# AdaLN products moved to the boundaries between sublayers, and the last AdaLN chunk computed in two halves

## The chip, the cores and the metric

The kernel runs on one core of a Trainium2 chip. The core has five engines that work side by side, each through its own instruction queue: TensorE (PE in the profile; its weight loads are shown as PEld), VectorE (DVE), ScalarE (ACT), GpSimd (POOL) and SyncE (SP, which here only issues DMAs). PE writes its results to PSUM; everything else lives in SBUF. The metric is the device time of one execution in microseconds (us); lower is better.

## What is computed

The reference is a trunk of two layers over 256 latent and 256 context tokens of width 1024. Each layer has a mixer (mLSTM, differential attention and a Fourier branch, merged by gates) and an FFN, and before each of these the stream is normed and modulated. The part that matters here is where the modulation comes from (AdaLN): a vector per stream (latent, context) times a 1024 x 6144 matrix per layer, cut in six.

```python
for l in range(DEPTH):
    ml = jnp.split((s_lat @ w_ada[l] + b_ada[l])[:, None, :], 6, axis=-1)
    mc = jnp.split((s_ctx @ w_ada[l] + b_ada[l])[None, None, :], 6, axis=-1)
    hl = _modulate(_rmsnorm(xl, norm_g[l, 0]), ml[0], ml[1])
    hc = _modulate(_rmsnorm(xc, norm_g[l, 0]), mc[0], mc[1])
    yl, yc = _mixer(hl, hc, ...)
    xl = xl + ml[2] * yl
    xl = xl + ml[5] * _swiglu(_modulate(_rmsnorm(xl, norm_g[l, 1]), ml[3], ml[4]), w_ffn_in[l], w_ffn_out[l])
    if need_ctx:
        xc = xc + mc[2] * yc
        xc = xc + mc[5] * _swiglu(_modulate(_rmsnorm(xc, norm_g[l, 1]), mc[3], mc[4]), w_ffn_in[l], w_ffn_out[l])
```

The second layer (l = 1) needs its mixer output and FFN for the 256 latent tokens alone.

## The kernel before

**Jobs.** The work is a list, `prog`, of jobs. A job is one weight tile of 512 KB: its DMA (`load`, L204), its split into a high part on ACT (`split_hi`, L214) and a low part on DVE (`split`, L224), and its matmuls, three for each f32 product (high by high, high by low, low by high). `run_all` goes through the list: before job i runs, the loads of all jobs up to i + 7 are written out (`AHEAD_LOAD`, L288), and the splits of up to three jobs ahead. Raw weight tiles have four buffers, so the load of job n + 4 waits until job n is split. Within a job, `yield` marks places where the side work of the moment (`side`, `tick`) may write out one of its steps, at a rate given by a number of steps over a number of jobs.

**What sets the order.** SP issues its DMAs in the order in which the program writes them. The other engines' instructions are ordered by a list scheduler, which takes whatever it holds to be ready, in the written order where several are; inside `chain` (L594 to L658) DVE and ACT too keep the written order, but not PE.

**Buffers.** A unit (`unit()`) is 4 KB a partition, and there are 32 of them, for the stream, the normed tokens, the activations and the AdaLN weights. The small PSUM tiles (`side_ps()`) have four buffers.

**AdaLN.** Layer 0's first chunk is made in the opening. The other five chunks of 2048 columns (layer 0: s = 1, 2; layer 1: s = 0, 1, 2) are objects of the class `Ada`. A chunk has eight products, one for each 128 rows k of the matrix; a product is four matmuls (j = 0 to 3) of the 128x32 vector columns by 128x512 of weights, each into its own 32 rows of one PSUM tile, at L363. Its weights are two units of 512 KB, one for j = 0, 1 and one for j = 2, 3 (L369). `steps` is the side work: a step loads one k, and every second step multiplies two products whose weights were loaded two and three steps before (a pair). At the end the bias is added (L373), and for s > 0 the rows go to DRAM in two DMAs (L377), from where the gates are read again in broadcast (`ada_gate`, L438). Layer 1's chunk 0 (`ada1`) is made during the FFN of layer 0, chunk 1 (`adab`) during the first ten jobs of layer 1 after the boundary, chunk 2 (`adac`) during the eight jobs of "dv".

**Boundaries.** `residual` closes a sublayer. Of its last output half, the last three weight tiles (four, in layer 1) are held back, so that the first token blocks (A) end early: their gate, residual sum, sum of squares (L472) and reciprocal root (L475 to L482) on ACT and DVE and their scaling (L487) run while PE multiplies the rest for the other blocks (B). Then `h_banks` transposes the normed blocks on PE (L502), applies scale and shift on ACT (L509, L515) and takes the low part on DVE (L518); a part is two token blocks. `first_jobs` runs the first three jobs of the next sublayer together (L647 to L649): their matmuls for the first part, with the second part's banks between, and then for the second part. There are three such boundaries: B1 (layer 0, mixer to FFN, near 833 us), B2 (layer 0 to layer 1, near 1213 us), both with two parts, and B3 (layer 1, mixer to FFN, near 1762 us), with one.

```python
                if not final:
                    bd().open()
                if len(B) == 2:
                    order = [(B[0], 0), (B[1], 0)] + [(B[0], i) for i in range(1, hold)] + [(B[1], i) for i in range(1, hold)]
```

Of the kernel before, what the change touches and what calls it, by code (L numbers as in the profile page):

```python
# [18 lines left out]
KB = D // 128  # L19
# [24 lines left out]
def tile_trunk(ctx: ExitStack, tc: tile.TileContext, x, c, cx, c_ctx, w_ada, b_ada, norm_g, w_in, ml_gate_b,  # L44
# [296 lines left out]
    class Ada:  # L341


        def __init__(self, l, s):
            self.l, self.s, self.rows = l, s, None

        def start(self):
            self.bias = cpool.tile([128, 512], F32, tag="abias", name=nm("ab"), bufs=2)
# [3 lines left out]
                                    b_ada[self.l, 2048 * self.s:2048 * self.s + 2048].rearrange("(j n) -> j n", j=4))  # L352
            self.ps = side_ps()

        def steps(self):
            self.start()
            raws = {}
            for i in range(KB + 2):
                if i >= 3 and i % 2:

                    for k in (i - 3, i - 2):
                        for j in range(4):
                            T.matmul(self.ps[32 * j:32 * j + 32, :], lhsT=s32[:, k, :], rhs=raws[k, j // 2][:, j % 2, :],  # L363
                                     start=(k == 0), stop=(k == KB - 1))
                if i < KB:
                    for hf in range(2):
                        raws[i, hf] = unit()
                        c0 = 2048 * self.s + 1024 * hf
                        nc.sync.dma_start(raws[i, hf].rearrange("p a n -> p (a n)"),  # L369
                                          w_ada[self.l, i * 128:i * 128 + 128, c0:c0 + 1024])  # L370
                yield
            self.rows = arow_pool()
            V.tensor_tensor(out=self.rows, in0=self.ps, in1=self.bias, op=ALU.add)  # L373
            if self.s > 0:
                self.scr = dpool.tile([2, 4, 512], F32, tag="ascr", name=nm("as"))
                for r in range(2):
                    nc.sync.dma_start(self.scr[r], self.rows[r:128:32, :])  # L377

    class AdaPart:

# [37 lines left out]
    def ada_cols(rows, js):  # L418

        ps = side_ps()  # L420
        for b in range(4):
            T.transpose(ps[:, b * 128:b * 128 + 128], rows[:, b * 128:b * 128 + 128], ident)
        pv = ps.rearrange("p (b q) -> p b q", b=4)
        res = []
        for j in js:
            o = cpool.tile([128, 2, KB], F32, tag="acol", name=nm("ac"), bufs=6)
            for jj in range(2):
                V.tensor_copy(o[:, :, 4 * jj:4 * jj + 4].rearrange("p r b -> p b r"),
                              pv[:, :, 32 * (j + jj):32 * (j + jj) + 2])
            res.append(o)  # L430
        return res
# [103 lines left out]
                for _ in range(n):  # L535
                    next(self.banks[i], None)

    def residual(st, key, xs, src, nk, acts, tbs, gate, bd, final=None):

        call(lambda: st.__setitem__(key, {tb: unit() for tb in tbs}))  # L540

        def evac(tb, ps, g, meanwhile=None):
            t = tmp()
            V.tensor_tensor(out=t, in0=ps, in1=gate()[tb // 2][:, g, :], op=ALU.mult)
            V.tensor_tensor(out=st[key][tb][:, g, :], in0=t, in1=xs()[tb][:, g, :], op=ALU.add)
            n = bd().nrm
            if g == 0:
                n.first(tb, st[key][tb][:, 0, :])
                return
            r = n.second(tb, st[key][tb][:, 1, :], meanwhile)  # L550
            if final:
                final(tb, st[key][tb], r)
            else:
                n.scale(tb, st[key][tb], r)
        proj_n(src[:, 0:512], nk, acts, tbs, lambda tb, ps: evac(tb, ps, 0))

        ps, held = {}, []

        def mm(tb, kt, job):
            for j in range(2):  # L560
                k = 2 * kt + j
                ah, al = act_k(acts(), k, tb * 128, tb * 128 + 128)
                T.matmul(ps[tb], lhsT=ah, rhs=job.hi[:, j, :], start=(k == 0), stop=False)  # L563
                T.matmul(ps[tb], lhsT=ah, rhs=job.lo[:, j, :], start=False, stop=False)  # L564
                T.matmul(ps[tb], lhsT=al, rhs=job.hi[:, j, :], start=False, stop=(k == nk - 1))  # L565

        nkt = nk // 2
        hold = W_BUFS if final or len(tbs) == 2 else HOLD
        A = tbs[:len(tbs) // 2]
        B = tbs[len(tbs) // 2:]  # L570

        def mk(kt):
            def run(job):
                if kt == 0:
                    ps.update({tb: main_ps() for tb in tbs})
                if kt < nkt - hold:
                    for tb in tbs:
                        mm(tb, kt, job)
                        yield
                    return  # L580
                held.append((kt, job))
                if kt < nkt - 1:
                    return
                nx = jobs_done()

                def ahead_hi(n):
                    if not final:
                        job_no(nx + n).split_hi()

                def ahead(n):  # L590
                    if not final:
                        upto("split", nx + 1 + n)
                if not final:
                    chain.enter_context(tc.manual_schedule(engines={ENG.DVE, ENG.Activation}))  # L594
                    job_no(nx + 1).in_units = hold == W_BUFS
                    job_no(nx + 2).in_units = True
                    ahead(1)
                for i, tb in enumerate(A):
                    if i == 0:
                        ahead_hi(2)  # L600
                    for q, jb in held:
                        mm(tb, q, jb)
                    with urgent():
                        evac(tb, ps[tb], 1, (lambda: ahead(2)) if i == 0 else None)
                    yield
                if not final:
                    bd().open()
                if len(B) == 2:
                    order = [(B[0], 0), (B[1], 0)] + [(B[0], i) for i in range(1, hold)] + [(B[1], i) for i in range(1, hold)]
                else:  # L610
                    order = [(B[0], i) for i in range(hold)]
                for n, (tb, i) in enumerate(order):
                    mm(tb, *held[i])
                    if tb == B[-1] and i == 0:
                        ahead_hi(3)
                    if i == hold - 1:
                        with urgent():
                            evac(tb, ps[tb], 1, (lambda: ahead(3)) if tb == B[0] else None)
                    if not final and len(order) - n <= 2 and len(bd().parts) == 2:
                        bd().bank(0, 1)  # L620
                    yield
            return run
        for kt in range(nkt):
            prog.append(Job(src[kt * 256:kt * 256 + 256, 512:1024], 2, 512, mk(kt)))

            prog[-1].ahead = min(AHEAD_SPLIT, nkt - 1 - kt)

    def first_jobs(bd, specs):

        jobs = []  # L630

        def run(job):
# [6 lines left out]
            for half in range(len(b.parts)):  # L639
                p = b.parts[half]  # L640
                n0, n1 = p[0] * 128, p[-1] * 128 + 128
                if half == 0:
                    b.bank(0, 4)
                for i, jb in enumerate(jobs):
                    for k in range(KB):
                        ah, al = act_k(b.h, k, n0, n1)
# [3 lines left out]
                        if k % 4 == 3:  # L650
                            yield
                    if half < len(b.parts) - 1:
                        if i:
                            b.bank(1, 2)
                    else:
# [675 lines left out]
    def plan(l, xget, fin, bd1, bd2, bdn):  # L1331
# [10 lines left out]
        nT = len(tbs)  # L1342
        hf = []
        ada = adas[l]

        def start():
            if l == 0:
# [100 lines left out]
        if l == 0:  # L1448
            opening_jobs(bd1, specs, parts)
        else:  # L1450
            first_jobs(bd1, specs)
        call(start)
        side("adab", ada[1].steps, 10, 10)
        proj_tt("dk", CDK, 0, True, nop)
        side("hf", lambda: fold_h(h(), len(segs), hf, st), 12 if l == 0 else 8, 7 * nT // 4)
        proj_tt("dq", CDQ, n0, True)
# [2 lines left out]
        proj_z(l, W, len(segs), hf, st)  # L1459
        proj_t(W[:, CGATE:CGATE + 16], h, 0, lambda ps: st.__setitem__("gps", ps), GateJob)  # L1460
        side("gates", lambda: ml_gates(l, st["gps"], st), 18, 8)
        side("adac", ada[2].steps, 10, 8)
        proj_nn("dv", CDV, ALL, cp)
        drain("gates")
        drain("adac")
# [31 lines left out]
            (sc,) = ada_cols(ada[2].rows, (0,))  # L1497
            bd2().scale = scale_cols(sc, vc["norm2"])
        call(gate1)
        residual(st, "x2", lambda: st["xr"], w_out[l], KB, lambda: st["yy"], tbs, lambda: st["gate1"], bd2)  # L1500
        specs = []
        for j in range(FB):
            ev = {}
# [7 lines left out]
            def evac_b(ps, ev=ev, j=j):  # L1511
                if j % 2 == 0:
# [6 lines left out]
                V.tensor_tensor(out=st["us"][1][j // 2][:, j % 2, n0:], in0=u[:, n0:], in1=hh, op=ALU.subtract)  # L1519
            specs += [(Job, w_ffn_in[l, :, 128 * j:128 * j + 128], evac_a),  # L1520
                      (Job, w_ffn_in[l, :, DFF + 128 * j:DFF + 128 * j + 128], evac_b)]
        first_jobs(bd2, specs[:3])
        if l == 0:
            def more():
                yield from adas[1][0].steps()
            side("ada1", more, 10, 36)
        for _, src, ev in specs[3:]:
            proj_t(src, lambda: bd2().h, n0, ev)
        if l == 0:
            drain("ada1")  # L1530

        def gate2():
            st["gate2"] = ada_gate(ada[2], 2, rs)
            if l == 0:
                cols1(1, bdn())
        call(gate2)
        residual(fin, l, lambda: st["x2"], w_ffn_out[l], FB, lambda: st["us"], tbs, lambda: st["gate2"], bdn,
                 finish if last else None)

    def cols1(l, bd):  # L1540
        shift1, scale1 = ada_cols(adas[l][0].rows, (0, 2))
        bd.scale, bd.shift = scale_cols(scale1, vcol[:, 32 * l:32 * l + 8]), shift1

    adas = [[Ada(l, s) for s in range(3)] for l in range(2)]
    fin = {}
    bds = {}

# [116 lines left out]
```

## Time and profile before

| | us |
|---|---|
| median of 3 runs | 1966.94 (1964.46 to 1972.05) |
| the profiled execution | 1967.22 |
| its span | 1965.5 |
| PE busy | 1910.6 |
| DVE busy | 1193.9 |
| ACT busy | 782.6 |
| L363, idle time before it put down to DMA | 0.9 (2 times) |

The span is the time from the first to the last instruction of the profiled execution. A row of the engine's timeline shows the start in us, the duration in us, engine, line, operation, output and inputs, and in brackets the idle time before it and what ended it. Matmuls are pipelined: a row's duration is longer than its distance to the next row, and the distance is what counts. A row of the chain shows the start, the time and what it was. A row of the windows shows the stretch and its length, then for each engine (PE, PEld, DVE, ACT, POOL) the busy time and the instructions, then the granted PE clock (1.00 is full), the busy share of the DMA engines and GB/s.

### The profile page before, as it was taken

How to read it: one execution, taken by the hardware profiler on the slowest of the kernel's cores; microseconds unless marked ns; L12 is line 12 of the kernel's file. 1: busy time of each engine (PE TensorE's matmuls, PEld its weight loads, DVE VectorE, ACT ScalarE, POOL GpSimd, SP SyncE). 2: the span in 40 equal slices, each digit the busy share in tenths (PEclk: the TensorE clock that was granted, in tenths of full speed). 3: DMA queues.
4: the chain of work that ended last, by engine and by line, in shares of the span. 5: the costliest groups of instructions: out<-in, count | busy, mean ns of one | idle time of the engine just before them, and what ended most of it. 6: DMA issues, size and time to landing. Idle time of an engine off the chain costs nothing.

```text
span 1965.5 us, 27681 instructions
## 1 busy us (share of the span) xinstructions
PE 1910.6 (97%) x10504; PEld 1589.3 (81%) x10504; DVE 1193.9 (61%) x2592; ACT 782.6 (40%) x1466; POOL 142.6 (7%) x164
## 2 busy tenths in 40 slices
PE   6999999999999999999999999999999999989998
PEld 4778788888777778888777887877878888889996
DVE  4797688852476457654333235676995477576655
ACT  3233466632344323352222224322773354345443
POOL 0231100000001110000000000160100010000000
PEclk8999999999999999999999999999999999999999
DMA  9647522224322224434443332668313563555664
GB/s 307 188 137 225 174 68 62 66 87 123 112 75 86 65 82 122 153 92 152 140 149 95 115 97 70 220 195 281 103 54 86 178 196 119 151 182 167 185 196 129
DMA packets 339894, 269.48 MB, mean 137 GB/s; under 512 B 17233, under 2 KB 296145, under 8 KB 339762
## 3 DMA queue, kind: packets, MB, share of 16 engines
q1 hardware_dynamic: 339040, 265.09, 44.8%
q10 hardware_dynamic: 722, 2.62, 0.3%
q8 instruction: 83, 1.36, 0.3%
q14 instruction: 49, 0.40, 0.1%
HBM read 264.73 MB, written 7.11 MB: 138 GB/s over the span
## 4 chain that ended last, share of the span: by engine, by line
PE 79%; DVE 10%; DMA 4%; ACT 4%; issue 2%; POOL 0%; SPq 0%; DVEq 0%; ACTq 0%; POOLq 0%
PE m L309 13%; PE m L311 13%; PE m L310 13%; PE m L330 6%; PE m L332 6%; PE m L331 6%; DVE wl L224 2%; DMA wr<-in_w_in_dram 2%; PE p L1149 2%; PE m L564 2%; PE m L565 2%; PE m L563 2%; PE p L1113 1%; PE p L363 1%; PE m L678 1%
## 5 line engine op out<-in xcount | busy, mean ns | idle before, releaser
L224 DVE TENSOR_TENSOR wl<-wr,wh 128x1024 fp32r<-128x1024 f32 x336 | 420.6, 1255 | 415.2 <-ACT wh L214 412.5
L309 PE MATMUL m<-u,wh 128*128 128x512 f32 (+1 forms) x1752 | 616.3, 352 | 4.2 <-DVE u L1213 2.5
L214 ACT CAST wh<-wr 128x1024 fp32r<-128x1024 f32 x336 | 351.5, 1049 | 651.3 <-issue 227.3
L311 PE MATMUL m<-u,wl 128*128 128x512 f32 (+1 forms) x1752 | 602.4, 344 | 2.5 <-DVE wl L224 2.5
L310 PE MATMUL m<-u,wh 128*128 128x512 f32 (+1 forms) x1752 | 601.8, 344 | 0.0
L309 PEld LDWEIGHTS m<-u,wh 128*128 128x128 f32 x1752 | 332.4, 190 | 57.6 <-issue 8.0
L311 PEld LDWEIGHTS m<-u,wl 128*128 128x128 f32 x1752 | 332.3, 190 | 43.0 <-DVE wl L224 4.0
L310 PEld LDWEIGHTS m<-u,wh 128*128 128x128 f32 x1752 | 332.5, 190 | 39.0 <-issue 3.1
L330 PE MATMUL m<-wh,u 128*128 128x512 f32 x532 | 215.1, 404 | 0.0
L332 PE MATMUL m<-wh,u 128*128 128x512 f32 x532 | 208.0, 391 | 0.0
L331 PE MATMUL m<-wl,u 128*128 128x512 f32 x532 | 208.0, 391 | 0.0
L330 PEld LDWEIGHTS m<-wh,u 128*128 128x128 f32 x532 | 100.0, 188 | 25.7 <-issue 6.2
L332 PEld LDWEIGHTS m<-wh,u 128*128 128x128 f32 x532 | 99.9, 188 | 21.1
L331 PEld LDWEIGHTS m<-wl,u 128*128 128x128 f32 x532 | 100.1, 188 | 20.6 <-issue 1.4
L1255 ACT ACTIVATE u<-p,s 128x512 f32<-128x512 f32 (+1 forms) x96 | 59.3, 617 | 40.0 <-DVE s L1254 37.8
L563 PE MATMUL m<-wh,u 128*128 128x512 f32 x180 | 70.2, 390 | 0.0
L565 PE MATMUL m<-wh,u 128*128 128x512 f32 x180 | 70.1, 389 | 0.0
L564 PE MATMUL m<-wl,u 128*128 128x512 f32 x180 | 70.0, 389 | 0.0
L1214 POOL TENSOR_TENSOR u<-u,t 128x256 f32<-128x256 f32 x32 | 42.5, 1327 | 327.5 <-DVE u L1213 316.3
L1517 DVE SCALAR_TENSOR_TENSOR t<-t,m 128x512 f32<-128x512 f32 (+1 forms) x44 | 24.4, 554 | 62.9 <-PE m L311 62.4
L1252 DVE TENSOR_REDUCE s<-p 128x1 f32<-128x512 f32 (+1 forms) x96 | 57.1, 595 | 7.6 <-PE p L1250 7.4
L1212 DVE TENSOR_TENSOR t<-m,cst 32x256 f32<-32x256 f32 x128 | 53.8, 420 | 3.7 <-ACT u L1370 1.4
(288 smaller groups left out, 2499.7 us busy)
## 6 DMA issues: line engine op xcount, KB each, us to landing
wr<-in_w_in_dram SPq DMA_DIRECT2D x176, 512.0 KB
wr<-in_w_ffn_in_dram SPq DMA_DIRECT2D x88, 512.0 KB
u<-in_w_ada_dram SPq DMA_DIRECT2D x80, 512.0 KB
wr<-in_w_ffn_out_dram SPq DMA_DIRECT2D x44, 512.0 KB
u<-in_w_ada_dram SPq DMA_DIRECT2D x32, 256.0 KB
wr<-in_w_br_da_dram SPq DMA_DIRECT2D x16, 512.0 KB
wr<-in_w_br_ml_dram SPq DMA_DIRECT2D x16, 512.0 KB
wr<-in_w_out_dram SPq DMA_DIRECT2D x16, 512.0 KB
```

Of the source, the lines that this page charges most:

```text
L214: S.copy(self.hi, self.raw)
L224: V.tensor_tensor(out=self.lo, in0=raw, in1=self.hi, op=ALU.subtract)
L309: T.matmul(ps[:, n0:], lhsT=job.hi[:, k, :], rhs=ah, start=(k == 0), stop=False)
L310: T.matmul(ps[:, n0:], lhsT=job.hi[:, k, :], rhs=al, start=False, stop=False)
L311: T.matmul(ps[:, n0:], lhsT=job.lo[:, k, :], rhs=ah, start=False, stop=(k == KB - 1))
L330: T.matmul(st[tb], lhsT=ah, rhs=job.hi[:, j, :], start=(k == 0), stop=False)
L331: T.matmul(st[tb], lhsT=ah, rhs=job.lo[:, j, :], start=False, stop=False)
L332: T.matmul(st[tb], lhsT=al, rhs=job.hi[:, j, :], start=False, stop=(k == nk - 1))
L563: T.matmul(ps[tb], lhsT=ah, rhs=job.hi[:, j, :], start=(k == 0), stop=False)
L564: T.matmul(ps[tb], lhsT=ah, rhs=job.lo[:, j, :], start=False, stop=False)
L565: T.matmul(ps[tb], lhsT=al, rhs=job.hi[:, j, :], start=False, stop=(k == nk - 1))
L1255: S.activation(p[:, m, :nk], sp[:, :nk], AF.Exp, bias=nb, scale=0.125, accum_out=d[:, m:m + 1])
```

## The change

`Ada` gets its loads and products as functions of their own, and a `preload`, which starts the chunk and loads its first four k. `residual` calls `preload` of a chunk right after it opens the boundary; `first_jobs` writes out the four products: with two parts, product 0 after the first part's banks, product 1 after the first of the three jobs' first halves, products 2 and 3 after the second; with one part, all four ahead of the banks. `steps` goes on with k = 4, in six steps in place of ten. B1 takes the first half of layer 1's chunk 0, B2 that of chunk 1. Layer 1's chunk 2 becomes two chunks of 1024 columns, `AdaHalf`: its product i holds two k (i and i + 4) by two column blocks, into the same four groups of 32 rows, and at the end the two sums are added. The first half chunk is made in "dv", in six steps, the second one wholly at B3. The number of matmuls and of loaded bytes stays.

```diff
     class Ada:
...
+        n, ahead = KB, 0
         def __init__(self, l, s):
-            self.l, self.s, self.rows = l, s, None
+            self.l, self.s, self.rows, self.raws = l, s, None, {}
...
+        def load(self, i):
+            for hf in range(2):
+                self.raws[i, hf] = unit()
+                c0 = 2048 * self.s + 1024 * hf
+                nc.sync.dma_start(self.raws[i, hf].rearrange("p a n -> p (a n)"),
+                                  w_ada[self.l, i * 128:i * 128 + 128, c0:c0 + 1024])
+        def product(self, i):
+            for j in range(4):
+                T.matmul(self.ps[32 * j:32 * j + 32, :], lhsT=s32[:, i, :], rhs=self.raws[i, j // 2][:, j % 2, :],
+                         start=(i == 0), stop=(i == self.n - 1))
+        def preload(self):
+            self.start()
+            self.ahead = 4
+            for i in range(4):
+                self.load(i)
         def steps(self):
-            self.start()
-            raws = {}
-            for i in range(KB + 2):
-                if i >= 3 and i % 2:
-                    for k in (i - 3, i - 2):
-                        for j in range(4):
-                            T.matmul(self.ps[32 * j:32 * j + 32, :], lhsT=s32[:, k, :], rhs=raws[k, j // 2][:, j % 2, :],
-                                     start=(k == 0), stop=(k == KB - 1))
-                if i < KB:
-                    for hf in range(2):
-                        raws[i, hf] = unit()
-                        c0 = 2048 * self.s + 1024 * hf
-                        nc.sync.dma_start(raws[i, hf].rearrange("p a n -> p (a n)"),
-                                          w_ada[self.l, i * 128:i * 128 + 128, c0:c0 + 1024])
+            if not self.ahead:
+                self.start()
+            for i in range(self.ahead, self.n + 2):
+                if i >= self.ahead + 3 and i % 2:
+                    self.product(i - 3)
+                    self.product(i - 2)
...
+            self.finish()
+        def finish(self):
...
+    class AdaHalf(Ada):
+        n = 4
+        def start(self):
+            self.bias = cpool.tile([128, 512], F32, tag="abias", name=nm("ab"), bufs=2)
+            G.memset(self.bias, 0.0)
+            self.c0 = 4096 + 1024 * self.s
+            for r in range(2):
+                nc.sync.dma_start(self.bias[r:64:32, :],
+                                  b_ada[self.l, self.c0:self.c0 + 1024].rearrange("(j n) -> j n", j=2))
+            self.ps = side_ps()
+        def load(self, i):
+            for b in range(2):
+                self.raws[i, b] = unit()
+                k = i + 4 * b
+                nc.sync.dma_start(self.raws[i, b].rearrange("p a n -> p (a n)"),
+                                  w_ada[self.l, k * 128:k * 128 + 128, self.c0:self.c0 + 1024])
+        def product(self, i):
+            for b in range(2):
+                for j in range(2):
+                    q = 32 * (2 * b + j)
+                    T.matmul(self.ps[q:q + 32, :], lhsT=s32[:, i + 4 * b, :], rhs=self.raws[i, b][:, j, :],
+                             start=(i == 0), stop=(i == 3))
+        def finish(self):
+            self.rows = arow_pool()
+            t = tmp()
+            S.copy(t[0:64, :], self.ps[64:128, :])
+            V.tensor_tensor(out=self.rows[0:64, :], in0=self.ps[0:64, :], in1=self.bias[0:64, :], op=ALU.add)
+            V.tensor_tensor(out=self.rows[0:64, :], in0=self.rows[0:64, :], in1=t[0:64, :], op=ALU.add)
+            if self.s > 0:
+                self.scr = dpool.tile([2, 2, 512], F32, tag="hscr", name=nm("hs"))
+                for r in range(2):
+                    nc.sync.dma_start(self.scr[r], self.rows[r:64:32, :])
...
     def ada_cols(rows, js):
         ps = side_ps()
+        n = 128 if max(js) else 64
         for b in range(4):
-            T.transpose(ps[:, b * 128:b * 128 + 128], rows[:, b * 128:b * 128 + 128], ident)
-        pv = ps.rearrange("p (b q) -> p b q", b=4)
+            T.transpose(ps[:, b * n:b * n + n], rows[0:n, b * 128:b * 128 + 128], ident[0:n, 0:n])
+        pv = ps[:, 0:4 * n].rearrange("p (b q) -> p b q", b=4)
...
-    def residual(st, key, xs, src, nk, acts, tbs, gate, bd, final=None):
+    def residual(st, key, xs, src, nk, acts, tbs, gate, bd, final=None, ada=None):
...
                     yield
                 if not final:
                     bd().open()
+                    ada().preload()
                 if len(B) == 2:
...
-    def first_jobs(bd, specs):
+    def first_jobs(bd, specs, ada):
...
@@ -640,7 +701,12 @@
                 p = b.parts[half]
                 n0, n1 = p[0] * 128, p[-1] * 128 + 128
                 if half == 0:
+                    if len(b.parts) == 1:
+                        for i in range(4):
+                            ada().product(i)
                     b.bank(0, 4)
+                    if len(b.parts) == 2:
+                        ada().product(0)
                 for i, jb in enumerate(jobs):
...
                         if k % 4 == 3:
                             yield
                     if half < len(b.parts) - 1:
+                        for q in ((1,), (2, 3), ())[i]:
+                            ada().product(q)
                         if i:
                             b.bank(1, 2)
...
         nT = len(tbs)
         hf = []
         ada = adas[l]
+        fill = adas[1][0] if l == 0 else ada[3]
...
         if l == 0:
             opening_jobs(bd1, specs, parts)
         else:
-            first_jobs(bd1, specs)
+            first_jobs(bd1, specs, lambda: ada[1])
...
-        side("adab", ada[1].steps, 10, 10)
+        side("adab", ada[1].steps, 10 if l == 0 else 6, 10)
...
+        side("adac", ada[2].steps, 10 if l == 0 else 6, 8)
...
-        residual(st, "x2", lambda: st["xr"], w_out[l], KB, lambda: st["yy"], tbs, lambda: st["gate1"], bd2)
+        residual(st, "x2", lambda: st["xr"], w_out[l], KB, lambda: st["yy"], tbs, lambda: st["gate1"], bd2, ada=lambda: fill)
...
-        first_jobs(bd2, specs[:3])
+        first_jobs(bd2, specs[:3], lambda: fill)
+        if l:
+            call(fill.finish)
         if l == 0:
             def more():
                 yield from adas[1][0].steps()
-            side("ada1", more, 10, 36)
+            side("ada1", more, 6, 36)
...
         def gate2():
-            st["gate2"] = ada_gate(ada[2], 2, rs)
+            st["gate2"] = ada_gate(ada[2], 2, rs) if l == 0 else ada_gate(fill, 0, rs)
             if l == 0:
                 cols1(1, bdn())
         call(gate2)
         residual(fin, l, lambda: st["x2"], w_ffn_out[l], FB, lambda: st["us"], tbs, lambda: st["gate2"], bdn,
-                 finish if last else None)
+                 finish if last else None, lambda: adas[1][1])
...
-    adas = [[Ada(l, s) for s in range(3)] for l in range(2)]
+    adas = [[Ada(0, s) for s in range(3)], [Ada(1, 0), Ada(1, 1), AdaHalf(1, 0), AdaHalf(1, 1)]]
```

More of the change, by code (lines that the diff above doesn't have):

```diff
@@ L353, in start @@
             self.ps = side_ps()
-        def steps(self):
-            self.start()
-            raws = {}
-            for i in range(KB + 2):
-                if i >= 3 and i % 2:
-                    for k in (i - 3, i - 2):
-                        for j in range(4):
-                            T.matmul(self.ps[32 * j:32 * j + 32, :], lhsT=s32[:, k, :], rhs=raws[k, j // 2][:, j % 2, :],
-                                     start=(k == 0), stop=(k == KB - 1))
-                if i < KB:
-                    for hf in range(2):
-                        raws[i, hf] = unit()
-                        c0 = 2048 * self.s + 1024 * hf
-                        nc.sync.dma_start(raws[i, hf].rearrange("p a n -> p (a n)"),
-                                          w_ada[self.l, i * 128:i * 128 + 128, c0:c0 + 1024])
+        def load(self, i):
[13 more added lines that the diff above has]
+                self.load(i)
+        def steps(self):
+            if not self.ahead:
[4 more added lines that the diff above has]
+                    self.product(i - 2)
+                if i < self.n:
+                    self.load(i)
                 yield
+            self.finish()
+        def finish(self):
             self.rows = arow_pool()
@@ L1461, in plan @@
         side("gates", lambda: ml_gates(l, st["gps"], st), 18, 8)
-        side("adac", ada[2].steps, 10, 8)
+        side("adac", ada[2].steps, 10 if l == 0 else 6, 8)
         proj_nn("dv", CDV, ALL, cp)
```

## The prediction, made before the result was known

> **What bounds the kernel now.** I read the head of the page first, then the chain that ended last, then the idle times of PE (TensorE) in order of time, and last the product line L363. The head gives the span, and PE as the bound:
>
> ```profile
> span 1965.5 us, 27681 instructions
> ...
> PE 1910.6 (97%) x10504; PEld 1589.3 (81%) x10504; DVE 1193.9 (61%) x2592; ACT 782.6 (40%) x1466; POOL 142.6 (7%) x164
> ...
> PE 79%; DVE 10%; DMA 4%; ACT 4%; issue 2%; POOL 0%; SPq 0%; DVEq 0%; ACTq 0%; POOLq 0%
> ```
>
> An instruction taken out of PE's row is worth its time where the chain lies on PE, and nothing where it lies on DVE. The moved work is line L363, two records for each of its 160 matmuls:
>
> ```profile
> L363 PE MATMUL p<-u,s x320: 592/592/617, 88.5 to 1378.7; 128*32 128x512 f32 x160
> ```
>
> The change sends 12 products (of four matmuls, eight records) to three boundaries: B1 (layer 0, mixer to FFN), B2 (layer 0 to layer 1), B3 (layer 1, mixer to FFN). PE's idle times there, in brackets, are the room for them:
>
> ```profile
> 839.46 0.39 PE L647 MATMUL m<-u,wh 128*128 128x256 f32 x1 [0.78 <-ACT u L509]
> 841.79 0.55 PE L502 MATMUL p<-cst,u 128*128 128x128 f32 x3 [1.82 <-DVE u L487]
> 861.11 0.50 PE L311 MATMUL m<-u,wl 128*128 128x512 f32 x1 [0.29 <-DVE wl L224]
> ...
> 1221.26 0.55 PE L502 MATMUL p<-cst,u 128*128 128x128 f32 x3 [1.82 <-DVE u L487]
> 1241.26 0.50 PE L311 MATMUL m<-u,wl 128*128 128x512 f32 x1 [0.95 <-DVE wl L224]
> ...
> 1765.16 2.82 PE L502 MATMUL p<-cst,u 128*128 128x128 f32 x12 [4.78 <-DVE u L487]
> 1777.52 0.39 PE L309 MATMUL m<-u,wh 128*128 128x256 f32 x1 [0.39 <-ACT wh L214]
> 1778.73 0.39 PE L309 MATMUL m<-u,wh 128*128 128x256 f32 x1 [0.71 <-ACT wh L214]
> ```
>
> Behind these holes the granted clock falls. In the windows below read PE's busy time, PEclk and, last, the share and rate of DMA:
>
> ```profile
> 836.20:839.70 3.50, 2.38 (x18) 2.18 (x18) 2.51 (x9) 1.47 (x4) 0.00 (x0) 1.00 0.11 34
> 839.70:843.10 3.40, 1.58 (x13) 1.38 (x13) 3.16 (x11) 3.40 (x9) 0.00 (x0) 1.00 0.00 0
> 843.10:846.50 3.40, 3.40 (x19) 3.40 (x18) 1.50 (x4) 3.40 (x9) 0.00 (x0) 0.51 0.00 0
> ...
> 1218.60:1222.00 3.40, 1.25 (x9) 1.04 (x10) 3.08 (x14) 3.40 (x9) 0.00 (x0) 1.00 0.00 0
> 1222.00:1225.40 3.40, 3.40 (x19) 3.40 (x18) 1.50 (x5) 3.40 (x9) 0.00 (x0) 0.50 0.00 0
> ```
>
> After a window with PE busy for 1.58 of 3.40 us the next runs at 0.51, which loses 3.40 x 0.49 = 1.67 us; at B2 it is 1.70 us. After 2.38 of 3.50 us nothing falls.
>
> **What is removed.** One pair of products in the FFN of layer 0:
>
> ```profile
> 939.48 0.39 PE L311 MATMUL m<-u,wl 128*128 128x512 f32 x1
> 939.80 1.92 PE L363 MATMUL p<-u,s 128*32 128x512 f32 x16
> 941.65 0.50 PE L309 MATMUL m<-u,wh 128*128 128x512 f32 x1
> 942.00 0.40 PE L310 MATMUL m<-u,wh 128*128 128x512 f32 x1
> ```
>
> Without it L309 would start 0.23 us after 939.48, and L310 0.23 us after that: 941.65 - 939.48 - 0.23 + 0.35 - 0.23 = 2.06 us for a pair. Six pairs leave the body. The chain tells which of them count:
>
> ```profile
> 981.43 1.85 PE p L363 x16
> ...
> 1262.86 1.85 PE p L363 x16
> 1270.23 1.06 ACT wh L214
> ...
> 1301.16 0.61 DVE ar L373
> ...
> 1321.35 0.50 PE p L311
> ...
> 1344.36 1.85 PE p L363 x16
> ...
> 1377.40 1.85 PE p L363 x16
> ```
>
> Two of four pairs go in the layer-0 FFN (the chain has the one at 939.80 and that at 981.43): 4.12 us. Of the four pairs of adab in layer 1 two go, but from 1270.23 to 1321.35 the chain runs over DVE, a load and POOL; only the pair at 1262.86 lies before that, so 2.06 us (bounds: 0, and 4.12 if DVE's chain moves up with PE). Of the four of adac between 1344.36 and 1377.40, all on the chain, two go: 4.12 us (at least 2.06, if the attention stage behind them hands part of it to DVE). In all 10.3 us.
>
> **When the data is there.** The sync queue (SP) works in the written order. preload comes when the last job of the residual is written out, behind the loads up to seven jobs ahead. The last of those waits for a split, and the moves below stand behind it:
>
> ```profile
> 833.52 0.37 SPq L204 DMA_DIRECT2D wr<-in_w_ffn_in_dram  x1
> 861.08 4.82 SPq L204 DMA_DIRECT2D wr<-in_w_ffn_in_dram  x4
> ...
> 1213.00 0.37 SPq L204 DMA_DIRECT2D wr<-in_w_in_dram  x1
> ...
> 1285.28 1.01 SPq L369 DMA_DIRECT2D u<-in_w_ada_dram  x2
> ...
> 1762.49 0.37 SPq L204 DMA_DIRECT2D wr<-in_w_ffn_in_dram  x1
> ```
>
> An issue takes about 0.5 us (1.01 for two). Two bias DMAs go ahead, so the first half of product 0 is issued at 833.52 + 0.37 + 1.1 = 835.0, and at 1214.5 and 1764.0. How long it flies is shown by the one place where products stand close behind their loads, the end of adab:
>
> ```profile
> 1288.80 1.06 PE L363 MATMUL p<-u,s 128*32 128x512 f32 x8
> 1289.80 0.39 PE L309 MATMUL m<-u,wh 128*128 128x256 f32 x1
> 1290.52 1.05 PE L363 MATMUL p<-u,s 128*32 128x512 f32 x4 [0.34 <-DMA u<-in_w_ada_dram]
> ...
> 1292.21 0.28 PE L309 MATMUL m<-u,wh 128*128 128x256 f32 x1
> 1292.42 1.05 PE L363 MATMUL p<-u,s 128*32 128x512 f32 x4
> 1293.40 0.38 PE L310 MATMUL m<-u,wh 128*128 128x256 f32 x1
> ...
> 1260.00:1270.00 10.00, 10.00 (x52) 6.89 (x51) 5.02 (x10) 1.32 (x2) 1.47 (x2) 1.00 1.08 360
> ```
>
> Issued at 1285.28, landed at 1290.5: at most 5.2 us, in a busy stretch; at least the 1.46 us that 512 KB take at 360 GB/s. I take 4 us, nearer the row. So the first half lands near 839.0, 1218.5 and 1768.0, and one more every 1.46 us: eight halves span about 12 us. Two things follow. B1 and B2 can take product 0 into the hole of 1.82 us, and the clock is kept (1.58 + 1.17 or more of 3.40 us busy). B3's hole of 4.78 us, the largest, ends at 1765.16, before anything has landed.
>
> **What a product costs at its landing.** The same rows show that PE's order isn't the written one there: a product was cut in two at its two loads, with other matmuls between. Half a product (x4) takes 1.05 us, a whole one (x8) 1.06: half the columns of the array stand idle. Half a product displaces 1293.40 - 1292.21 - 0.12 = 1.07, and 0.1 for the slower restart: 1.17 us. So a product is worth 1.03 us in a pair, 1.2 alone (1289.80 - 1288.80 and both changes), 2.34 cut. Landings 1.46 us apart are further apart than a half is long, so whatever ranks above the waiting work is cut.
>
> B1: product 0 cut, 2.34 - 1.82 in the hole = 0.52; product 1, ahead of jobs 1 and 2, cut, 2.34; products 2 and 3, behind job 1's first half, by then landed, a pair, 2.06. Sum 4.92; less the clock 1.67 and the wait at 861.11 of 0.29, which a later PE no longer has: +2.96. B2: 4.92 - 1.70 - 0.95 = +2.27. B3: all four rank ahead of everything, eight halves, 9.36, less 0.39 + 0.71: +8.26. In all +13.5.
>
> On the clock the Trainium skill, "TensorE: Matmul & The Clock Gate", section "HAM oscillation — how this bites in real kernels", speaks against the change: it gives "no PE-idle gaps >~3.4µs" as the rule, and no gap of B1 or B2 is longer than 1.82 us. By that rule filling them would win no clock, and the sum would be 3.4 us higher. The rows above show the fall behind gaps of 0.78 and 1.82 us, so I keep the row.
>
> At nothing I cost these. The loads: DMA share is 0.00 to 0.11 in B1 and the next load is issued at 861.08, 20 us after the move begins; without that cover each costs 1.46 us. Their buffers: at 833 about 21 of 32 units are in use (4 of the stream, 4 normed, 8 of h, 2 of a weight, some 3 not yet released), 8 are needed; were they not free, the loads would come later, which is a rival below. The PSUM bank held from product 0 on, while the norm's transposes use all four: 0 to 1 us at each boundary, by the hole at 839.46; I take 0, since ACT, not the banks, sets their pace. The finish of the half chunk (a copy on ACT, an add on DVE, two stores that hold SP): 0 to 1.2 us by the 0.61 of L373; 0 taken, since PE leads there.
>
> **The sum.** 1967.22 (the profiled execution, 1.7 above its span, 0.3 above the median 1966.94) - 10.3 + 13.5 = 1970.4 us. The three terms at the boundaries eat what the body gains.
>
> **The rivals.**
> Whole products: they land together or behind a backlog, as 1288.80 did. Then product 0 is hidden entirely, product 1 costs 1.2 and the pair 2.06: B1 3.26 - 1.96 = 1.3, B2 0.6, B3 4.12 - 1.1 = 3.0; 4.9 - 10.3 = -5.4: 1961.8. For it: every earlier pair is whole. Against: those were loaded long before.
> PE waits for the data (the slower side): PE keeps the written order, or an order made for earlier landings. At B3 it would stand at product 0 before the 12 transposes until the last half at 1768.0 + 7 x 1.46 = 1778.2, and then 1.2: 14 us late, +13 with the 1.1 gone. At B1 and B2 product 0 would hold the first jobs until about 842: some 31 short matmuls of 0.12 us late, 3.7, and 3.3 for the others: +7 each. 27 - 10.3: 1984. It decides if landings come over 1 us after the place PE has for them. Against: only 0.34 us at 1290.52.
> The move misses the holes: buffers come late, products run whole behind the boundary, 12 x 1.03 = 12.4 less the later waits 0.29 + 0.95 + 1.1: +10.1 - 10.3: 1967.
> More is won: whole products, and DVE's chain after 1270 moves up with both pairs (2.06), with up to 4 us from the 2 MB that leave its saturated DMA (share 1.08 above): 1956.
>
> **How the numbers follow.** Cut 0.46 (1966 to 1976 by itself), whole 0.25, PE waits 0.12, misses 0.09, more 0.08. The likeliest gives 1970.4. The range is 1957 to 1979: the floor leaves out half of the last rival, the ceiling most of the third; the bounds of adac and of the clock (2.06 + 3.4 above 1970.4, and 3 for the costs taken as 0) reach 1979. Faster by over 0.5% (under 1957.1), which is about what a measurement of this kernel can tell from no change: 0.09, from the last rival and the edge of the second. Slower (over 1976.8): 0.18, the third rival and the forecast's upper edge. Same: 0.73.
>
> **What would show it.** In the trace after: L363 with x4 groups at the boundaries (cut) or x8 and x16 (whole), an idle time of PE released by the DMA of w_ada at a product (waits), PEclk near 1.0 in the stretches 843 and 1222 (clock kept), the 4.78 us hole of B3 still there, and one pair fewer ahead of the DVE chain of layer 1. I am wrong if the loads are issued before the last weight load of the boundary, so that B3's hole is filled, or if PE idles at a product.

## The result, and the profile after

The changed kernel takes 1983.98 us (median of 4 runs, 1983.76 to 1984.28) against 1966.74 (1964.46 to 1972.05) beside it: a ratio of 1.0082, 95% interval 1.0068 to 1.0096. It is slower by 0.8%; the forecast was 1970.4 and the range ended at 1979. One run of the late kernel (the second experiment below), of 6685.79 us, is left out of its median, range and ratio.

The head of the changed kernel's page: span and busy time by engine.

```profile
span 1981.9 us, 27692 instructions
...
PE 1917.2 (97%) x10504; PEld 1585.9 (80%) x10504; DVE 1196.9 (60%) x2595; ACT 784.5 (40%) x1468; POOL 141.1 (7%) x165
```

The span grew by 16.4 us, PE's busy time by 6.6, so PE's idle time by 9.8. Where it idles stands in PE's list of waits, cut to the three boundaries (sum, times, longest):

```profile
PE p L367 <- DMA u<-in_w_ada_dram: 4.5, 1, 4.5
...
PE p L367 <- ACT u L568: 2.5, 1, 2.5
...
PE p L423 <- DMA u<-in_w_ada_dram: 9.4, 2, 9.2
```

L367 and L423 are the products (L363 before). Each boundary now has a wait at its first product. SP's and PE's rows of the timeline show how it comes about; first B1, then B2, then B3:

```profile
834.80 1.08 SPq L353 DMA_DIRECT2D ab<-in_b_ada_dram  x2
835.93 5.00 SPq L362 DMA_DIRECT2D u<-in_w_ada_dram  x8
...
837.40 0.39 PE L714 MATMUL m<-u,wh 128*128 128x256 f32 x1 [1.26 <-DVE u L577]
842.25 3.15 PE L367 MATMUL p<-u,s 128*32 128x512 f32 x8 [4.47 <-DMA u<-in_w_ada_dram]
845.33 0.39 PE L715 MATMUL m<-u,wl 128*128 128x256 f32 x1
...
1219.71 4.31 SPq L362 DMA_DIRECT2D u<-in_w_ada_dram  x8
...
1224.10 3.16 PE L367 MATMUL p<-u,s 128*32 128x512 f32 x8 [2.53 <-ACT u L568]
...
1767.87 4.91 SPq L416 DMA_DIRECT2D u<-in_w_ada_dram  x8
...
1772.92 3.40 PE L423 MATMUL p<-u,s 128*32 128x512 f32 x8 [9.18 <-DMA u<-in_w_ada_dram]
1776.25 0.90 PE L561 MATMUL p<-cst,u 128*128 128x128 f32 x3
```

At B1 PE reaches product 0 at 837.8, 1.9 us after its first load was issued, and stands until 842.25. At B3 it reaches it at 1763.7, before the load is issued at all. Nothing else is done meanwhile, though at B3 the 12 transposes (L561) hang on other data. At B2 the profile puts the wait down to ACT; the first experiment tells whether ACT or the load held PE there.

The two halves of product 0 stand together in the queue (x8), but the second has a wait of its own, which the row hides, as PE is still busy with the first. The second half's weight loads on PE (PEld, here of the vector columns) show it, at B1, B2 and B3:

```profile
843.48 0.18 PEld L367 LDWEIGHTS p<-u,s 128*32 128x32 f32 x4 [1.04 <-DMA u<-in_w_ada_dram]
...
1225.34 0.19 PEld L367 LDWEIGHTS p<-u,s 128*32 128x32 f32 x4 [1.10 <-DMA u<-in_w_ada_dram]
...
1774.40 0.19 PEld L423 LDWEIGHTS p<-u,s 128*32 128x32 f32 x4 [1.29 <-DMA u<-in_w_ada_dram]
```

So the first product takes 3.15 to 3.40 us in place of 1.06: the second half starts 1.23 to 1.48 us behind the first, and a half takes 1.92 us at half clock (the one-product kernel below has one by itself). PE's busy time thus holds some waiting, too. The windows (as in the prediction: PE's busy time first, granted clock third from last) show the half clock at B1 and B2:

```profile
838.60:842.00 3.40, 0.00 (x0) 0.00 (x0) 2.24 (x12) 2.90 (x8) 0.00 (x0) 0.50 1.01 339
842.00:845.40 3.40, 3.15 (x9) 0.48 (x9) 2.43 (x7) 3.29 (x8) 0.00 (x0) 0.51 1.02 407
...
1220.80:1224.20 3.40, 0.49 (x3) 0.32 (x5) 2.45 (x8) 1.32 (x4) 0.00 (x0) 1.00 1.00 331
1224.20:1227.60 3.40, 3.40 (x10) 0.64 (x10) 3.15 (x12) 3.40 (x9) 0.00 (x0) 0.50 1.03 420
```

To size each term I cut the span at rows that both kernels have: the first high matmuls of `first_jobs` and the last matmuls of the Fourier branch. The view of one source line gives, behind the three durations, its first and last start. Before:

```profile
L647 PE MATMUL m<-u,wh x32: 274/283/415, 834.6 to 859.8; 128*128 128x256 f32 x32
...
L647 PE MATMUL m<-u,wh x32: 277/283/415, 1214.2 to 1239.3; 128*128 128x256 f32 x32
...
L964 PE MATMUL m<-u,u x64: 273/275/276, 1701.5 to 1736.9; 128*128 128x127 f32 x64
...
L647 PE MATMUL m<-u,wh x8: 283/283/284, 1771.5 to 1776.6; 128*128 128x256 f32 x8
```

After:

```profile
L713 PE MATMUL m<-u,wh x32: 278/283/387, 835.5 to 869.3; 128*128 128x256 f32 x32
...
L713 PE MATMUL m<-u,wh x32: 278/283/387, 1219.4 to 1251.2; 128*128 128x256 f32 x32
...
L1032 PE MATMUL m<-u,u x64: 273/275/275, 1704.2 to 1740.6; 128*128 128x127 f32 x64
...
L713 PE MATMUL m<-u,wh x8: 278/283/283, 1783.0 to 1792.7; 128*128 128x256 f32 x8
```

B1 and B2 are first to last start; the FFN lies between B1's last and B2's first, layer 1 between B2's last and the last Fourier matmul, B3 from there to its last start.

| stretch, us | before | after | difference | forecast |
|---|---|---|---|---|
| B1 | 25.2 | 33.8 | +8.6 | +2.96 |
| FFN, layer 0 | 354.4 | 350.1 | -4.3 | -4.12 |
| B2 | 25.1 | 31.8 | +6.7 | +2.27 |
| layer 1 | 497.6 | 489.4 | -8.2 | -6.18 |
| B3 | 39.7 | 52.1 | +12.4 | +8.26 |

The differences make +15.2; 0.9 more lies ahead of B1 and 0.3 behind B3. The body gave a little more than was forecast, the boundaries took twice what was forecast.

### The profile page after: what moved, and what is told of

It reads as the page before. It is cut to its first block, busy times and chain, and to the rows that moved or that the text cites. A ratio compares the mean times of both kernels' runs of the same rounds, so it can differ in the third digit from the quotient of the medians.

```text
span 1981.9 us, 27692 instructions
## 1 busy us (share of the span) xinstructions
PE 1917.2 (97%) x10504; PEld 1585.9 (80%) x10504; DVE 1196.9 (60%) x2595; ACT 784.5 (40%) x1468; POOL 141.1 (7%) x165
## 4 chain that ended last, share of the span: by engine, by line
PE 79%; DVE 10%; DMA 4%; ACT 4%; issue 2%; SPq 0%; POOL 0%; DVEq 0%; ACTq 0%; POOLq 0%
PE m L309 13%; PE m L311 13%; PE m L310 13%; PE m L330 6%; PE m L332 6%; PE m L331 6%; DVE wl L224 2%; PE p L1217 2%; DMA wr<-in_w_in_dram 2%; PE m L623 2%; PE m L622 2%; PE m L624 2%; PE p L367 2%; PE p L1181 1%; DVE t L1280 1%
## 5 line engine op out<-in xcount | busy, mean ns | idle before, releaser
L311 PE MATMUL m<-u,wl 128*128 128x512 f32 (+1 forms) x1752 | 601.8, 343 | 3.3 <-DVE wl L224 3.3
L311 PEld LDWEIGHTS m<-u,wl 128*128 128x128 f32 x1752 | 331.7, 189 | 43.9 <-DVE wl L224 5.0
```

Of the source, the lines that this page charges most:

```text
L311: T.matmul(ps[:, n0:], lhsT=job.lo[:, k, :], rhs=ah, start=False, stop=(k == KB - 1))
```

## The experiments

Theory W: each product has a fixed place in PE's order, too early for its weights, and PE stands there. The names of the theories are those of the expectations. The six kernels are edits of the changed one.

**The products read data that is there.**

```diff
+    res = cpool.tile([128, 512], F32, tag="res", name="res")
+    V.memset(res, 0.001)
...
-    rhs=self.raws[i, j // 2][:, j % 2, :]
+    rhs=res if i < self.ahead else self.raws[i, j // 2][:, j % 2, :]
```

> The first four products of the three boundary chunks multiply a resident tile of the constant 0.001 in place of their weights (so these weights are left out of the result); their loads are still issued, but nobody waits for them. Theory W (PE stands in its queue at a product whose weights are still in flight: 4.5, 2.5 and 9.2 us at the three boundaries, and works at the low clock behind it): all of this goes, 1956 to 1964 us. Rival A (at B1 and B2 it is the PSUM buffer, freed late by ACT, that product 0 waits for, and only B3 waits for weights): 1968 to 1974. Rival C (the products' own time, cut in halves at the boundary, is the loss): stays within 4 us of 1984.

Measured: 1957.25 us (1957.06 to 1958.72), ratio 0.995 (0.9933 to 0.9966). Its rows, as above:

```profile
L717 PE MATMUL m<-u,wh x32: 279/283/387, 835.7 to 861.8; 128*128 128x256 f32 x32
...
L717 PE MATMUL m<-u,wh x32: 279/283/387, 1211.9 to 1238.0; 128*128 128x256 f32 x32
...
L1036 PE MATMUL m<-u,u x64: 273/275/275, 1691.7 to 1726.9; 128*128 128x127 f32 x64
...
L717 PE MATMUL m<-u,wh x8: 278/283/283, 1756.8 to 1766.5; 128*128 128x256 f32 x8
```

B1 falls from 33.8 to 26.1 us, B2 from 31.8 to 26.1, B3 from 52.1 to 39.6: 25.9 of the 26.7 us between the two medians. The loads are still issued at the same places, so neither they nor the products' own time make the kernel slow; the waiting does, with the low clock behind it. C is out, and so is A: product 0 still takes its PSUM buffer, ACT does the same work, and the wait at B2 is gone. At B1 PE has the same groups in the same order as in the changed kernel. The four products of a boundary then cost 0.9, 1.0 and nothing. PE's row at B3 shows why nothing:

```profile
1749.92 3.64 PE L426 MATMUL p<-res,s 128*32 128x512 f32 x32
...
1755.28 1.20 PE L565 MATMUL p<-cst,u 128*128 128x128 f32 x9 [1.24 <-DVE u L550]
```

All four run in 3.64 us where the hole of 4.78 was; 1.24 us of idle time are left.

**The products behind the first jobs.** All four are written out after the three jobs.

```diff
-                    if len(b.parts) == 1:
-                        for i in range(4):
-                            ada().product(i)
...
             chain.close()
+            for i in range(4):
+                ada().product(i)
```

> The changed kernel with the four products written behind the three first jobs of each boundary, the loads where the change has them. W: the weights have landed by then, every product is whole; the stretches away from the boundaries keep what they gained (13 us by the two traces), the boundaries pay 12 x 1.03 = 12.4 us less the waits that a later PE does not have: 1963 to 1969. Rival S (the loads, the held PSUM bank or the units disturb the norm of the boundary, whoever multiplies): 1975 or more.

Measured: 1961.16 us (1958.9 to 1967.88), ratio 0.9971 (0.9958 to 0.9984), 1.8 us below what W gave. The old holes are back, as at B3:

```profile
PE p L561 <- DVE u L546: 4.8, 1, 4.8
```

No new wait comes with them, and the loads at the boundary disturb nothing that shows: S is out. The products are hidden by nothing here, and the kernel is still 5.6 us faster than before (1966.77 beside it). In the FFN stretch, where they now stand, it has 353.3 us (last start 862.0, next first start 1215.3): 3.2 more than the changed kernel's 350.1, less than the 4.1 of four products by 1.03. PE's later wait of 0.3 us at L311 is gone; the other 0.6 stay open.

**Only B3's products behind the first jobs.** The same edit for the boundary with one part.

> The changed kernel with B3's four products alone written behind its first jobs. W: B3 costs about 3 us in place of the 13 to 14 us by which the two traces part there: 1971 to 1975. C: 1980 or more.

Measured: 1976.19 us (1971.17 to 1976.91), ratio 1.0039 (1.0024 to 1.0054): 7.8 less than the changed kernel, so C is out. It is 1.2 above the upper end of what W gave, but not for B3: from the last Fourier matmul to the last start B3 takes 1783.0 - 1742.7 = 40.3 us, 0.6 more than before, and 2.7 more than in the changed kernel lie behind it, where the four products now stand. Together that is about W's 3. Layer 1 (491.5) and B2 (32.7), which the edit leaves alone, are 2.1 and 0.9 us longer than in the changed kernel's trace; why is open. W's waits at the other two boundaries are there:

```profile
PE p L367 <- DMA u<-in_w_ada_dram: 4.0, 1, 4.0
...
PE p L367 <- DMA u<-in_w_ada_dram: 3.3, 1, 3.3
```

**The loads one job earlier.** The preload moves from behind the first blocks of the residual to the first of its held jobs.

```diff
+                if kt == nkt - 4 and not final:
+                    ada().preload()
                 if kt < nkt - hold:
...
                     bd().open()
-                    ada().preload()
```

> The changed kernel with preload called at the start of the fourth last job of the residual, so that its loads stand about 14 to 20 us earlier in SP's queue; the products stay where they are in the written order. W: landed in time, the holes are filled: 1954 to 1964. A: B3's 9.2 us and 2 us of B1 go, B2's 2.5 us stays: 1966 to 1973. S: the loads now push the last weight tiles of the residual: 1980 or more.

Measured: 1961.79 us (1958.86 to 1962.6), ratio 0.9968 (0.9955 to 0.9982). SP and PE at B1, from the timeline, and two windows:

```profile
815.61 4.23 SPq L362 DMA_DIRECT2D u<-in_w_ada_dram  x8
...
835.89 0.39 PE L715 MATMUL m<-u,wh 128*128 128x256 f32 x1 [1.30 <-DVE u L577]
836.21 1.06 PE L367 MATMUL p<-u,s 128*32 128x512 f32 x8
...
835.40:838.80 3.40, 2.91 (x21) 1.03 (x21) 2.45 (x8) 1.21 (x4) 0.00 (x0) 1.00 0.20 58
838.80:842.20 3.40, 3.40 (x24) 1.48 (x23) 3.15 (x13) 3.40 (x8) 0.00 (x0) 1.00 0.00 0
```

Product 0 stands behind the same matmuls as in the changed kernel (L715 here is L714 there), but with its weights loaded 20 us earlier it runs at once, whole, and the clock stays at 1.00. So the landing doesn't move the place, and at B2 no wait for ACT is left either; A and S are out. B1 and B2 take 26.2 us each, 1.0 and 1.1 more than before. B3 still pays, from the last Fourier matmul to the last start 1770.7 - 1727.1 = 43.6 us, 3.9 above before:

```profile
1743.68 4.94 SPq L416 DMA_DIRECT2D u<-in_w_ada_dram  x8
...
1750.16 1.37 PE L423 MATMUL p<-u,s 128*32 128x512 f32 x8
1751.73 1.05 PE L423 MATMUL p<-u,s 128*32 128x512 f32 x4 [0.20 <-DMA u<-in_w_ada_dram]
...
1758.17 1.05 PE L423 MATMUL p<-u,s 128*32 128x512 f32 x4 [0.28 <-DMA u<-in_w_ada_dram]
1759.15 1.53 PE L561 MATMUL p<-cst,u 128*128 128x128 f32 x12
```

Here the half products come one for each landing, paced by the data at (1758.17 - 1751.73) / 5 = 1.29 us for a half, and all transposes stand behind them, as was forecast for B3. In the changed kernel three transposes stand ahead of product 1 (the row at 1776.25). So a product's place does differ between two kernels; within one it doesn't move when the data is late.

**B3's loads earlier still.** On the early kernel, the preload of the third boundary moves to the second job of the residual's first half.

```diff
                 if kt == 0:
                     st.update({tb: main_ps() for tb in tbs})
+                if kt == 1 and hook:
+                    hook()
```

> The early kernel (loads one job earlier) with the loads at the third boundary issued some 7 us earlier still, at the second job of the residual's first half. Theory W (the products stand too early for their weights): in the early kernel the six half products waited 0.2 us each and ran one by one ahead of the transposes; with the weights there in time they stand as pairs or fill the hole of 4.78 us, no product at this boundary waits, and the stretch from the end of the Fourier projections to the first jobs falls from 34.7 us to 31-32: 1957.5 to 1960 us, against 1961.8 of the early kernel. Rival Q: 4 MB more in front of the residual's and the output weights' loads stall the residual jobs themselves; the stretch stays at 34 us or above and the time is 1961 to 1966 us. If the planner sets the products in the same places whatever the loads do, the gain is the 1.4 us of waits alone, about 1960.4 us.

Measured: 1965.06 us (1963.52 to 1968.87), ratio 0.9991 (0.998 to 1.0001): 3.3 us slower than the early kernel, as rival Q has it, and not the 1957.5 to 1960 of W. B3 takes 1773.7 - 1726.3 = 47.4 us in place of 43.6.

```profile
1734.57 4.83 SPq L418 DMA_DIRECT2D u<-in_w_ada_dram  x8
1740.17 39.51 SPq L204 DMA_DIRECT2D wr<-in_w_ffn_in_dram  x9
...
1751.66 1.04 ACT L214 CAST u<-wr 128x1024 fp32r<-128x1024 f32 x1 [7.78 <-DMA wr<-in_w_ffn_in_dram]
...
1749.33 3.64 PE L425 MATMUL p<-u,s 128*32 128x512 f32 x32
1756.66 0.90 PE L563 MATMUL p<-cst,u 128*128 128x128 f32 x3 [3.69 <-DVE u L548]
1761.77 2.18 PE L563 MATMUL p<-cst,u 128*128 128x128 f32 x9 [4.21 <-DVE u L548]
```

As W has it, the products are now as in the first experiment, 3.64 us without a wait. But the FFN's weights are issued behind them, at 1740.17; ACT, which keeps the written order here, stands 7.78 us at the split of one of them, the norm's chain on ACT and DVE is queued behind it, and PE's idle time comes back as 3.69 + 4.21 us. A wait of PE for AdaLN weights became a wait of ACT for FFN weights.

**One product, two loads.** At B1 and B2 only product 0 is preloaded, at the place of the changed kernel; B3's products stand behind its first jobs.

```diff
-            self.ahead = 4
-            for i in range(4):
+            self.ahead = 4 if self.n == 4 else 1
+            for i in range(self.ahead):
                 self.load(i)
...
```

> At the first two boundaries the preload takes one product's weights (two loads instead of eight) at the place of the changed kernel, and one product stands between the norm and the first jobs; the other three go back into the fused jobs, and the third boundary's products stand behind its first jobs. Theory S (eight loads issued within 5 us share the DMA engines, so that even the first lands late): the first product's weights land 3.5 to 4.5 us after their issue, the wait at the first boundary falls from 4.5 us to 2-2.5 and at the second from 2.5 to below 1. Rival F (the time from issue to landing is fixed, whatever is queued with it): landing stays at about 6 us and the wait at 4-4.5 us. The time itself, between 1966 and 1974 us, tells little: fewer products are taken out of the fused jobs.

Measured: 1971.67 us, in a single run. At B1, and at B2:

```profile
835.05 0.91 SPq L362 DMA_DIRECT2D u<-in_w_ada_dram  x2
...
841.44 1.92 PE L367 MATMUL p<-u,s 128*32 128x512 f32 x4 [4.54 <-DMA u<-in_w_ada_dram]
...
1223.42 1.92 PE L367 MATMUL p<-u,s 128*32 128x512 f32 x4 [3.37 <-DMA u<-in_w_ada_dram]
```

With two loads in place of eight the first half still lands 6.3 us after its issue at B1, and the waits, 4.54 and 3.37 us, are no shorter than the 4.47 and 2.53 of the changed kernel. So S is out: the late landing isn't queueing behind the other six loads. F is right for B1; that the flight is a fixed time isn't shown, as at B2 it is about 1 us shorter.

## Why the prediction was wrong

**The step that failed** is the one that gave PE something else to do until the data is there: "PE's order isn't the written one there: a product was cut in two at its two loads", and from it "whatever ranks above the waiting work is cut". It was drawn from one place, the end of adab at 1290.52, where PE, too, stood, for 0.34 us. What the runs show in its place: the order is part of the kernel, and PE stands in it until the data lands, 4.47, 2.53 and 9.18 us long. The resident, the early and the changed kernel have product 0 at B1 behind the same matmuls, with weights that were there, that had long landed, and that landed 4.5 us late; without the waits 25.9 us are gone. The third rival had the mechanism and, by 27 - 10.3, the time (1984 forecast, 1983.98 measured), and got 0.12. That the times agree to the hundredth is luck: the boundaries took 27.7 us for its 27, the body gave 12.5 for 10.3, and 1.2 lie outside both. It said that it decides if landings come over 1 us after PE's place; the forecast itself had the first half at 839.0 for a hole that opened at 841.79 - 1.82 = 839.97, while PE's place for it in the changed kernel is ahead of that, at 837.8, and at B3 it had the first half at 1768.0, after all 12 transposes.

**The landing** was mis-sized, but is the smaller part. From issue to the first half of product 0 it was forecast at 4 us; the trace has 6.2 at B1 (835.93 to 842.1), at most 4.4 at B2 and 5.0 at B3. The second half followed 1.2 to 1.5 us later, for 1.46. With 4 us PE would still have stood 2.1, 2.1 and 8.1 us (835.93 + 4 - 837.8 at B1, and so on). The place of the loads on SP, behind the last weight load, was right at all three.

**What was removed** was right in size: -4.3 for 4.12 in the FFN. Layer 1 gave 8.2 for 6.18; that is the upper bound of 4.12 for adab with the 4.12 of adac, as if DVE's chain had moved up with both pairs. No run took one of the pairs away by itself. The one-product kernel, with three of these four products back in layer 1, has 1738.5 - 1246.5 = 492.0 us there, 2.6 more than the changed kernel, for 3.1 by 1.03 each; but the kernel with only B3's products moved has 491.5 with the same work in this stretch as the changed one. So it stays argued. The resident kernel has 1726.9 - 1238.0 = 488.9 us in that stretch, so the gain doesn't hang on the waits.

**What the products cost.** Half a product took 1.05 us at B3 of the early kernel, as forecast. B1's +8.6 holds 1.9 us more idle time (4.47 against 0.78 + 1.82). The products there take 7.9 us from row to row (3.1, 1.0, 1.0 and 2.8), for 4.1 by 1.03 each, as their halves land about 1.3 us apart and the first runs at half clock; the 1.7 us of half clock that the kernel before had at B1 are gone. B3's +12.4 holds 4.6 us more idle time and 2.3 under the first product (3.40 for 1.06), which is its second half's landing and the half clock.

**B3's hole** could not be filled by loads issued there, as forecast; it grew from 4.78 to 9.18. That four products fit into it for nothing, the resident kernel shows.

**The clock** fell as the rows of before had said, but it was not kept, since the hole wasn't filled: 0.50 and 0.51 in the windows above. In the early kernel, where it was filled, both windows are at 1.00. No run isolates the 1.7 us estimated for it at B1 and B2. On the rule of the Trainium skill that was weighed there, "TensorE: Matmul & The Clock Gate", section "HAM oscillation — how this bites in real kernels", B2 disagrees again: its gaps are 1.22 and 2.53 us, none over 3.4, and the next window ran at 0.50.

**Costs taken as nothing.** The buffers, the PSUM bank and the loads' share of the DMA cost nothing that shows: the resident kernel keeps all three and its boundaries take 0.9, 1.0 and -0.1 us. The second rival, whole products at 1961.8, is what the early kernel measures, 1961.79, with 1.0, 1.1 and 3.9 us at the boundaries for 1.3, 0.6 and 3.0 forecast; that the totals meet so closely is luck again, as its body gave about 1 us more than the 10.3 forecast.

## What to carry to other kernels

An instruction put into a hole is worth something only if its data is there when its engine gets to it: take the issue of the load from the trace, add the longest flight that the trace shows, and compare with the place in the queue, which doesn't move when the data is late. Where they cross, the price is the wait, the clock behind it and the work itself. Either the work goes further back or the loads go further up; here both gained 22 us or more on the changed kernel (1961.16 and 1961.79). Moving loads up has its own limit: each goes ahead of others on the issuing queue, so look who needs those first; nine microseconds more at one boundary lost 3 again.

## What had not been expected of the hardware

Two loads of 512 KB with one weight tile ahead of them did not land faster than eight: the first of them was there 6.3 us (B1) and at most 5.2 us (B2, issued at 1218.19) after its issue, with eight 6.2, at most 4.4 and 5.0 us. The view of DMA traffic in the one-product kernel, 833 to 845 us in slices of 0.3 us:

```profile
GB/s 0 0 0 0 0 97 215 290 254 321 335 271 169 150 205 218 246 246 232 259 300 287 219 219 205 191 164 96 55 41 14 0 0 0 0 0 0 0 0 0
```

Up to about 836.6 this is a weight tile of the FFN; the rest are the two AdaLN loads, at 150 to 300 GB/s to about 841, then less until 842.3, while eight of them reach 407 GB/s (windows above). The Trainium skill, "DMA: Bandwidth & Descriptors", section "Anatomy of one DMA — SWDGE (gpsimd) path", fits 2.0 us and bytes at 436 GB/s for DMAs that GpSimd issues; an estimate from it is 3.2 us for 512 KB, half of the 6.3 that these loads, issued by SP, show at B1. What limits them isn't settled by these runs.
